# Sample attention's key dots at the output projection, its values at the memory query's projection, in a hybrid decoder layer

## The chip, the cores and the metric

One core of a Trainium2 chip runs the whole layer as one program. Its engines are TensorE (PE in the profile; PEld is its weight load), VectorE (DVE), ScalarE (ACT), GpSimd (POOL) and SyncE (SP), which issues the ordinary DMAs; gathers are issued by GpSimd. The metric is device time in microseconds (us), from the runs of the program on the chip.

## The reference, cut to what matters

The layer serves 1024 prompt tokens and 8 sample tokens with the same weights, in float32:

```
h = RMSNorm(x)
x = x + W_out(sigmoid(g1) * SSD(h) + sigmoid(g2) * RWKV7(h))
x = x + MemCrossAttn(RMSNorm(x), mem_k, mem_v)
x = x + PEER(RMSNorm(x))
```

The change is in the third line, for the samples only. Each of the 8 sample rows has a memory of its own (cache_mem_k, cache_mem_v: 256 tokens, 4 heads of 256):

```
q = (h @ w_mq).reshape(b, L, MEM_HEADS, MEM_HD)
s = einsum('blhd,bmhd->bhlm', q, mem_k) * MEM_HD ** -0.5
prob = softmax(s)
o = einsum('bhlm,bmhd->blhd', prob, mem_v)
return o @ w_mo
```

PEER picks, per token, 16 experts for each of 8 heads, and needs one row of 1024 numbers from each of two tables per expert: U for a dot with the token, V for the weighted sum.

## The kernel before, in words

The prompt goes through `front(gi)` in four groups of two blocks of 128 tokens (gi 0 to 3; the text counts them from first to fourth). A front is: input norm, the z projection (L499), the convolution stage (six weight blocks of x, B, C, L562), the SSD scan over chunks, the RWKV branch with its projections, inverse and scan (`scan`, L892), and then `rest` (L1034): output projection `project(I["w_out"][0], mT)`, memory norm, the memory query's projection (L1082), memory attention of the prompt (from L1111 on), the projection w_mo, the norm before PEER, and eight heads of the projection w_pq with the choice of experts (`Best`, L420 to L460).

The experts of the group before are worked off beside a front. A U row is a gather (L1512 on POOL) and a dot on VectorE (L1516, in two instructions, the second of which reads out the sum); a V row is a gather and a scaled addition (L1568). Both land in the pool of rows "U", seven buffers. Each row is 128 partitions of 4 KB, 0.524 MB.

The samples ride along with different groups: their memory query is projected in the second group's `rest` (into `smp["q"]`), their attention `sample_attention` (L1445) runs in the third group, and their w_mo rows and experts follow there, reading `smp["o"]`. `sample_attention` is a generator of 17 steps. The first eight each load one sample's keys in two tiles of 128 x 1024 (L1457), spread the query over the partitions with two TensorE products into the tiles pc, and make eight dots of 256 columns on VectorE (L1516, key tile w by pc, result into sat). Then the softmax (L1474 to L1480) and two tiles of probabilities, filled with zeros by GpSimd (L1486). The next eight each load one sample's values (L1457) and add four products on TensorE into pc. The seventeenth copies out the result and transposes it into `smp["o"]`.

`aside_satt(n)` (L495) takes n steps of the generator where it is called, in the third group alone. `SATT = (0, 3)` takes none per weight block of the z projection and three per block of the convolution stage, so all seventeen steps stand in the convolution stage.

Weights come as two tiles of 128 x 4 x 256 per block of 256 output columns (`weights`, L254), from the pool "w", which has five buffers. The sample's key and value tiles come from the same pool. All these loads go through SyncE in a fixed order.

What decides the order of instructions on each engine is the scheduler of the recording layer: code that stands earlier has priority, and at each point the scheduler, by its own model of durations, puts the most urgent instruction that it holds for ready. The result is a fixed order per engine; on the chip, each engine waits for its next instruction's inputs. So a front's instructions have priority over the expert rows that stand behind it in the code, and the rows fill what the scheduler takes for gaps.

Of the kernel before, what the change touches and what calls it, by code (L numbers as in the profile page):

```python
# [25 lines left out]
NQ3, NG4, NXA, NK1, NU, NUT, NVS, NW, NAC = 26, 6, 2, 5, 7, 9, 6, 5, 1  # L26
NQ3B, NSC = 5, 3
ORDER = 0
SATT = (0, 3)
MPOS = 2  # L30
SPLIT = (0,)
LATE_SLOTS = ((), tuple(range(48, 108)))
# [12 lines left out]
def decode_layer(ctx, tc, I, O):  # L45
# [33 lines left out]
    def qw():  # L79
        return t("qw", [P, 2, TMAX + NS], 4)  # L80
# [7 lines left out]
    def f2():  # L88
        return t("f2", [P, 512], 4)
# [5 lines left out]
    def pp():  # L95
        return pst("pp", 2)
# [17 lines left out]
    def copy(out, in_, scale=None, bias=None):  # L114
        if bias is not None:
            S.activation(out, in_, AF.Identity, scale=scale if scale is not None else 1.0, bias=bias)
        else:
            S.activation(out, in_, AF.Copy, scale=scale if scale is not None else 1.0)  # L118
# [71 lines left out]
    def col(name, i, n=1):  # L190
        return cols[:, spots[name] + i:spots[name] + i + n]
# [59 lines left out]
    def weights(w, c0, n=256, split=False):  # L251
        x = Weights()
        for i in range(2):
            load(x.half[i][:, :, :n], w[i * 512:(i + 1) * 512, c0:c0 + n].rearrange("(k p) c -> p k c", p=P))  # L254
        return parts(x) if split else x
# [24 lines left out]
    def parts(wt):  # L280

        def row():
            return t("U", [P, D], n_u(), F32R).rearrange("p (k x) -> p k x", k=4)

        hi, lo = [], []
        for i, w in enumerate(wt.half):
            hi.append(row())
            copy(hi[i], w)
            lo.append(row() if i else wtile(F32R))
            V.tensor_tensor(lo[i], w, hi[i].bitcast(F32), op=OP.subtract)  # L290
        return [tuple(x[k // 4][:, k % 4, :] for x in (hi, lo)) for k in range(8)]
# [30 lines left out]
    def by_channel(wt, j, h, n, p):  # L322
        for k in range(8):
            if isinstance(h, Parts):
                three(p[:, :n], [x[:, j * P:(j + 1) * P] for x in wt[k]], h.of(k, slice(0, n)), k == 0, k == 7)
            else:
                mm(p[:, :n], wt.of(k, slice(j * P, (j + 1) * P)), h[k // 2][:, k % 2, :n], k == 0, k == 7)

    def by_token(wt, h, t0, n, p, nw=256):
        for k in range(8):  # L330
            if isinstance(h, Parts):
                three(p[:n, :nw], h.of(k, slice(t0, t0 + n)), wt[k], k == 0, k == 7)
            else:
                mm(p[:n, :nw], h[k // 2][:, k % 2, t0:t0 + n], wt.of(k, slice(0, nw)), k == 0, k == 7)
# [127 lines left out]
    def front(gi):  # L462
# [12 lines left out]
        def src_x(i):  # L475
            return I["x_prompt"][0, (b0 + i) * P:(b0 + i + 1) * P, :] if i < nb else I["x_sample"][:, 0, :]
# [18 lines left out]
        def aside_satt(n):  # L495
            for _ in range(n if sc_ else 0):
                next(satt)

        for i in range(4):  # L499
            wt = weights(w_in, Z0 + i * 256, split=sa)  # L500
            aside_satt(SATT[0])
            s2 = slice(i * 256, i * 256 + 256)
            for b, (t0, n) in enumerate(body):
                p = pp()
                by_token(wt, hT, t0, n, p)
                th = f2()
                S.activation(th[:n, :256], p[:n, :256], AF.Tanh, scale=0.5)
                if b < nb:
                    V.scalar_tensor_tensor(mg[b][:n, s2], th[:n, :256], 1.0, p[:n, :256], op0=OP.add, op1=OP.mult)  # L509
                else:  # L510
                    V.scalar_tensor_tensor(th[:n, :256], th[:n, :256], 1.0, p[:n, :256], op0=OP.add, op1=OP.mult)
                    V.tensor_tensor(mg[b][:n, s2], th[:n, :256], mg[b][:n, s2], op=OP.mult)
# [48 lines left out]
        xb = [q3() for _ in range(6)]  # L561
        for i in range(6):  # L562
            wt = weights(w_in, XBC0 + i * 256, split=sa)
            aside_satt(SATT[1])
            for j in range(2):
                ct = 2 * i + j
                p = pp()
                by_channel(wt, j, hT, TT_, p)
                acc = f2()

                def cw(k):
                    return col("conv_w", k * 12 + ct)

                copy(acc[:, :TP], p[:, :TP], scale=cw(3), bias=col("conv_b", ct))
                if sa:
                    copy(smp["raw"][:, ct, :], p[:, TP:TT_])
                copy(halo[:, ct, :], p[:, TP - 3:TP])
                for k in range(3):
                    V.scalar_tensor_tensor(acc[:, 3 - k:TP], p[:, :TP - 3 + k], cw(k), acc[:, 3 - k:TP],  # L579
                                           op0=OP.mult, op1=OP.add)  # L580
                V.tensor_tensor(acc[:, 0:3], acc[:, 0:3], hc[:, ct, :], op=OP.add)
                th = f2()
                S.activation(th[:, :TP], acc[:, :TP], AF.Tanh)
                V.scalar_tensor_tensor(xb[i][:, j, :TP], th[:, :TP], 1.0, acc[:, :TP], op0=OP.add, op1=OP.mult)
        aside_satt(17)
        if last:
            p = tp()
            T.transpose(p[:36, :P], halo.rearrange("p c i -> p (c i)"), ident)
# [445 lines left out]
        def rest(bl):  # L1034
# [4 lines left out]
            mg_ = [mg[b] for b in bl] + mg[nb:]  # L1039
            body = [(i * P, P) for i in range(nl)] + ([(TP, NS)] if sm else [])  # L1040

            def project(w, src, smp_src=None):

                for i in range(4):
                    wt = weights(w, i * 256)
                    s2 = slice(i * 256, i * 256 + 256)
                    for b, (t0, n) in enumerate(body):
                        p = pp()
                        if b == nl and smp_src:
                            by_token(wt, smp_src, 0, n, p)  # L1050
                        else:
                            by_token(wt, src, t0, n, p)
                        V.tensor_tensor(mg_[b][:n, s2], p[:n, :256], mg_[b][:n, s2], op=OP.add)

            mT = [qw() for _ in range(4)]
            for b, (t0, n) in enumerate(body):
                to_cols(mg_[b][:n, :], n, mT, t0)
            for b, (t0, n) in enumerate(body):
                load(mg_[b][:n, :], src_x(bl[b] if b < nl else nb))
            project(I["w_out"][0], mT)  # L1060

            def norm(scale_cb):
                ss = t("ss", [P, 4], 4)
# [17 lines left out]
            qT = [q3() for _ in range(4)]  # L1081
            for i in range(4):  # L1082
                wt = weights(I["w_mq"][0], i * 256)
                for j in range(2):
                    p = pp()
                    by_channel(wt, j, h2, TT_, p)
                    copy(qT[i][:, j, :TP], p[:, :TP])
                    if sm:
                        copy(smp["q"][:, 2 * i + j, :], p[:, TP:TT_])
            if sm:  # L1090
                load(smp["x1"], mg_[nl][:NS, :])
                body = body[:nl]
# [630 lines left out]

    late = []
    chosen = front(0)
    sample_recurrences()
    for gi in range(1, len(GROUPS)):
        ahead = front(gi)
        z = experts(prompts(chosen), GATHERED[gi - 1])
        late += [x for i, x in enumerate(z) if i not in GATHERED[gi - 1]]  # L1730
        samples(chosen)
        chosen = ahead
# [70 lines left out]
```

## Time and profile before

| | |
|---|---|
| runs, median of 3 | 4701.04 us (4698.99 to 4721.07) |
| the profiled execution | 4729.15 us, span 4727.4 us |
| VectorE busy | 3697.7 us, 78% of the span |
| TensorE busy | 3534.4 us, 75% |
| GpSimd busy | 2501.9 us, 53% |
| ScalarE busy | 1351.2 us, 29% |
| DMA | 1369.20 MB, mean 290 GB/s; gathers (queue 0) 948.03 MB |

Busy time is time in instructions that compute; register, semaphore and DMA-issuing instructions don't count, except that GpSimd's gathers do. A busy TensorE is not TensorE at its peak, since its matmuls are pipelined. The DMA share is the mean busy share of 16 DMA engines and can read a little above 1. In the chain of waits, each piece is what the next one waited for, followed back from the last instruction; "issue" is time in which an engine waited for nothing that the profile shows.

### The profile page before, as it was taken

How to read it: one execution, taken by the hardware profiler on the slowest of the kernel's cores; microseconds unless marked ns; L12 is line 12 of the kernel's file. 1: busy time of each engine (PE TensorE's matmuls, PEld its weight loads, DVE VectorE, ACT ScalarE, POOL GpSimd, SP SyncE). 2: the span in 40 equal slices, each digit the busy share in tenths (PEclk: the TensorE clock that was granted, in tenths of full speed). 3: DMA queues.
4: the chain of work that ended last, by engine and by line, in shares of the span. 5: the costliest groups of instructions: out<-in, count | busy, mean ns of one | idle time of the engine just before them, and what ended most of it. 6: DMA issues, size and time to landing. Idle time of an engine off the chain costs nothing.

```text
span 4727.4 us, 56327 instructions
## 1 busy us (share of the span) xinstructions
PE 3534.4 (75%) x18278; PEld 2706.4 (57%) x18278; DVE 3697.7 (78%) x7765; ACT 1351.2 (29%) x3489; POOL 2501.9 (53%) x2059
## 2 busy tenths in 40 slices
PE   7889875779886786788785884387976885338998
PEld 6778764557565565366574673265655743235555
DVE  5662287998878679988886699888766797998888
ACT  5545322133123221133132221132222215233322
POOL 0000035665656645564666657855545477774664
PEclk9987877888865887788757886588757897559999
DMA  4342588899978998899989987899869878988998
GB/s 123 99 130 73 173 280 318 269 320 344 337 260 283 354 339 275 318 323 318 349 269 353 340 280 272 281 328 312 287 217 357 310 239 312 344 311 326 406 406 352
DMA packets 609103, 1369.20 MB, mean 290 GB/s; under 512 B 86124, under 2 KB 332296, under 8 KB 608800
## 3 DMA queue, kind: packets, MB, share of 16 engines
q0 software_dynamic: 260352, 948.03, 56.0%
q1 hardware_dynamic: 348456, 417.57, 26.5%
q8 instruction: 145, 2.38, 0.2%
q14 instruction: 150, 1.23, 0.1%
HBM read 1335.60 MB, written 29.90 MB: 289 GB/s over the span
## 4 chain that ended last, share of the span: by engine, by line
DVE 32%; PE 30%; DMA 15%; issue 12%; ACT 5%; POOL 5%; SPq 1%; another core or an unknown queue 0%; POOLq 0%; DVEq 0%; ACTq 0%
PE pp L112 16%; DVE U L1516 10%; PE pc L112 8%; DVE acc L1568 5%; POOL U L1512 4%; DMA U<-in_expert_v_dram,idx 4%; DMA U<-in_expert_u_dram,idx 3%; PE pg L112 2%; PE pv L112 2%; DVE q3b L450 2%; DMA w<-in_w_in_dram 1%; PE tp L112 1%; DMA q<-kt_d 1%; DVE vs L1616 1%; DVE f L579 1%
## 5 line engine op out<-in xcount | busy, mean ns | idle before, releaser
L1512 POOL DMA_INDIRECT U<-in_expert_u_dram,idx x1024 | 1298.6, 1268 | 732.4 <-issue 189.8
L1516 DVE CUSTOM_DVE_ANT_0 U<-U,xa 128x1024 f32<-128x1024 f32 x1032 | 1267.9, 1239 | 115.3 <-DMA U<-in_expert_u_dram,idx 106.5
L1512 POOL DMA_INDIRECT U<-in_expert_v_dram,idx x768 | 925.8, 1205 | 724.7 <-DVE acc L1568 183.1
L1568 DVE SCALAR_TENSOR_TENSOR acc<-U,cf,acc 128x1024 f32<-128x1024 f32 x708 | 924.0, 1305 | 98.6 <-DMA U<-in_expert_v_dram,idx 85.1
L112 PE MATMUL pp<-qw,w 128*128 128x256 f32 (+2 forms) x2872 | 745.8, 413 | 151.2 <-issue 40.9
L112 PEld LDWEIGHTS pp<-qw,w 128*128 128x128 f32 x2872 | 591.3, 218 | 277.1 <-issue 110.8
L112 PE MATMUL pp<-w,qw 128*128 128x256 f32 (+1 forms) x2528 | 633.9, 405 | 117.9 <-DVE g L509 30.0
L112 PEld LDWEIGHTS pp<-w,qw 128*128 128x128 f32 (+1 forms) x2528 | 484.5, 195 | 247.2 <-DVE g L509 34.1
L112 PE MATMUL pc<-vs,cs 128*128 128x512 f32 x510 | 200.1, 447 | 35.8 <-ACT vs L118 19.9
L112 PE MATMUL pp<-q,w 128*128 128x128 f32 (+1 forms) x1024 | 196.0, 350 | 16.6 <-DMA w<-in_w_pq_dram 8.8
L112 PEld LDWEIGHTS pp<-q,w 128*128 128x128 f32 x1024 | 169.1, 210 | 33.0 <-ACT q L118 10.5
L121 POOL TENSOR_TENSOR q3b<-q3b,q3b 128x400 f32<-128x400 f32 (+1 forms) x130 | 154.6, 1202 | 57.3 <-DVE q3b L450 55.1
L112 PE MATMUL pp<-vs,cs 128*128 128x512 f32 x510 | 172.9, 393 | 0.0
L112 PE MATMUL pc<-rst,q 64*64 64x64 f32 x1024 | 170.5, 305 | 1.6 <-issue 1.0
L112 PE MATMUL pg<-q,q 64*128 64x128 f32 (+1 forms) x384 | 108.5, 441 | 79.5 <-DMA q<-kt_d 39.9
L304 PE MATMUL tp<-ident,g 128*128 128x128 f32 (+1 forms) x296 | 62.2, 346 | 138.5 <-DVE g L1018 52.2
L112 PE MATMUL pc<-g,q 128*64 128x64 f32 x1024 | 138.8, 316 | 16.2 <-issue 12.4
L112 PEld LDWEIGHTS pc<-vs,cs 128*128 128x128 f32 x510 | 93.5, 188 | 91.0 <-ACT vs L118 36.2
L112 PEld LDWEIGHTS pg<-q,q 64*128 64x128 f32 (+1 forms) x384 | 81.6, 273 | 101.0 <-DMA q<-kt_d 42.6
L112 PE MATMUL pc<-q,q 64*128 64x128 f32 (+1 forms) x512 | 102.1, 343 | 47.7 <-ACT q L118 27.8
L304 PEld LDWEIGHTS tp<-ident,g 128*128 128x128 f32 (+1 forms) x296 | 44.0, 183 | 157.3 <-issue 55.9
L112 PEld LDWEIGHTS pc<-rst,q 64*64 64x64 f32 x1024 | 114.4, 188 | 29.9 <-issue 3.2
(506 smaller groups left out, 6336.6 us busy)
## 6 DMA issues: line engine op xcount, KB each, us to landing
w<-in_w_in_dram SPq DMA_DIRECT2D x248, 512.0 KB
U<-in_expert_v_dram SPq DMA_DIRECT2D x128, 512.0 KB
w<-in_w_pq_dram SPq DMA_DIRECT2D x80, 512.0 KB
w<-in_w_out_dram SPq DMA_DIRECT2D x40, 512.0 KB
w<-in_w_mq_dram SPq DMA_DIRECT2D x40, 512.0 KB
w<-in_w_mo_dram SPq DMA_DIRECT2D x40, 512.0 KB
U<-in_expert_u_dram,idx POOLq DMA_INDIRECT x1024
U<-in_expert_v_dram,idx POOLq DMA_INDIRECT x768
```

Source lines behind the costliest of these rows:

```text
L112: T.matmul(out, a, b, start=first, stop=last)
L121: G.tensor_tensor(out, a, b, op=op)
L304: T.transpose(p[:, j * P:j * P + n], x[:, c * P:(c + 1) * P], ident[:n, :n])
L450: V.tensor_tensor(oh[:n], iota50[:n, None, :].to_broadcast([n, 8, NCAND]), posf[:n, h, k8].unsqueeze(2).to_broadcast([n, 8, NCAND]), op=OP ...
L579: V.scalar_tensor_tensor(acc[:, 3 - k:TP], p[:, :TP - 3 + k], cw(k), acc[:, 3 - k:TP], op0=OP.mult, op1=OP.add)
L1512: G.indirect_dma_start(out=dst, out_offset=None, in_=table, in_offset=bass.IndirectOffsetOnAxis(ap=idx, axis=0))
L1516: V.tensor_tensor_reduce(out=u, in0=u, in1=x, scale=1.0, scalar=0.0, op0=OP.mult, op1=OP.add, accum_out=out)
L1568: V.scalar_tensor_tensor(z["acc"], v, cf, z["acc"], op0=OP.mult, op1=OP.add)
L1616: V.tensor_scalar(rb[:, a, :], iota, by[:, 1, t0 + a:t0 + a + 1], by[:, 2, t0 + a:t0 + a + 1], op0=OP.is_equal, op1=OP.mult)
```

## The change

All three calls of `aside_satt` in the z projection and the convolution stage go, and the numbers SATT with them. `project` gets a parameter: with it, the output projection takes two steps behind each of its four weight blocks, eight in all, which are the key steps. The memory query's projection takes two behind each of its four blocks, which are the softmax and the eight value steps, and what is left follows behind its last block. Nothing else is edited.

```diff
-SATT = (0, 3)
...
         for i in range(4):
             wt = weights(w_in, Z0 + i * 256, split=sa)
-            aside_satt(SATT[0])
             s2 = slice(i * 256, i * 256 + 256)
...
         for i in range(6):
             wt = weights(w_in, XBC0 + i * 256, split=sa)
-            aside_satt(SATT[1])
             for j in range(2):
...
-        aside_satt(17)
         if last:
...
-            def project(w, src, smp_src=None):
+            def project(w, src, smp_src=None, aside=0):
 
                 for i in range(4):
                     wt = weights(w, i * 256)
+                    aside_satt(aside)
                     s2 = slice(i * 256, i * 256 + 256)
...
-            project(I["w_out"][0], mT)
+            project(I["w_out"][0], mT, aside=2)
...
             for i in range(4):
                 wt = weights(I["w_mq"][0], i * 256)
+                aside_satt(2)
                 for j in range(2):
                     p = pp()
                     by_channel(wt, j, h2, TT_, p)
                     copy(qT[i][:, j, :TP], p[:, :TP])
                     if sm:
                         copy(smp["q"][:, 2 * i + j, :], p[:, TP:TT_])
+            aside_satt(17)
             if sm:
```

In the orders that follow, line numbers of the change lie a few below those of before (L1516 is L1515 there, L579 is L576, L1457 is L1456). ISA rows with w and sat are the key dots (the row with sat alone reads out the sum), ISA rows with U and act the U rows' dots, L1568 (L1567) the V rows.

VectorE in the convolution stage of the third group, before (L579 and L584 are the convolution, L453 and L460 the choice of experts of the second group):

```order
L584 SCALAR_TENSOR_TENSOR q_2478_13164<-f_2523_13341,f_2522_13334 128x256
L579 SCALAR_TENSOR_TENSOR f_2525_13353<-pp_13344,cols,f_2525_13353 128x253
L460 TENSOR_TENSOR gate_10585<-gate_10585,gsum_11259 128x64
L453 TENSOR_REDUCE q3b_10964<-q3b_11224 128x8
L1568 SCALAR_TENSOR_TENSOR acc_12204<-U_12928,cf_12085,acc_12204 128x1024
L453 TENSOR_REDUCE q3b_10964<-q3b_11228 128x8
L1516 ISA w_13309,sat_13186<-w_13309,pc_13314 128x256
L1516 ISA sat_13186 128x1
```

The same place of the change, at the same V row (U_12928):

```order
L576 SCALAR_TENSOR_TENSOR f_2502_13266<-pp_13257,cols,f_2502_13266 128x255
L1567 SCALAR_TENSOR_TENSOR acc_12204<-U_12925,cf_12085,acc_12204 128x1024
L459 TENSOR_TENSOR gate_10585<-gate_10585,gsum_11259 128x64
L578 TENSOR_TENSOR f_2502_13266<-f_2502_13266,hc_13154 128x3
L452 TENSOR_REDUCE q3b_10964<-q3b_11224 128x8
L452 TENSOR_REDUCE q3b_10964<-q3b_11228 128x8
L1567 SCALAR_TENSOR_TENSOR acc_12204<-U_12928,cf_12085,acc_12204 128x1024
L581 SCALAR_TENSOR_TENSOR q_2479_13165<-f_2503_13273,f_2502_13266 128x256
```

The dots are gone, and the convolution has come a column block further at the same V row. No dot is left in the stage.

SyncE from the last scan load (tx) of the third group on, before:

```order
L909 DMA tx_15842<-td_188 32x16x32 x2
L1059 DMA g_2430_12954<-in_x_prompt_dram 128x1024
L1534 DMA out_dram<-acc_17691 128x1024
L254 DMA w_16191<-in_w_out_dram 128x4x256
L1059 DMA g_2431_12955<-in_x_prompt_dram 128x1024
L254 DMA w_16214<-in_w_out_dram 128x4x256
L1557 DMA acc_24033<-x_d 128x1024
L254 DMA w_16215<-in_w_out_dram 128x4x256
L254 DMA w_16293<-in_w_mq_dram 128x4x256
```

And in the change:

```order
L905 DMA tx_15587<-td_188 32x16x32 x2
L1056 DMA g_2430_12954<-in_x_prompt_dram 128x1024
L1456 DMA w_15922<-in_cache_mem_k_dram 128x1024
L1056 DMA g_2431_12955<-in_x_prompt_dram 128x1024
L253 DMA w_15957<-in_w_out_dram 128x4x256
L253 DMA w_15958<-in_w_out_dram 128x4x256
L1456 DMA w_15961<-in_cache_mem_k_dram 128x1024
L1533 DMA out_dram<-acc_17691 128x1024
L1456 DMA w_15962<-in_cache_mem_k_dram 128x1024
L1456 DMA w_15977<-in_cache_mem_k_dram 128x1024
L1456 DMA w_15978<-in_cache_mem_k_dram 128x1024
L1556 DMA acc_24033<-x_d 128x1024
```

Key tiles now stand between the residual rows and the output weights, four for two weight tiles. The value tiles stand in the same way among the w_mq weights. Before the tx loads, the change fetches two weight tiles and three key tiles ahead, where before five weight tiles stood.

VectorE at the output projection of the third group (L1053 adds a block of it to the residual), before:

```order
L1533 SCALAR_TENSOR_TENSOR acc_17691<-acc_17691,ssf_18478,pv_18483 128x512 x2
L1053 TENSOR_TENSOR g_2430_12954<-pp_16170,g_2430_12954 128x256
L1516 ISA U_18495,act_18378<-U_18495,xa_18376 128x1024
L1516 ISA act_18378 128x1
L1516 ISA U_18498,act_18378<-U_18498,xa_18376 128x1024
```

And in the change (L1050 is the same addition):

```order
L1515 ISA U_18504,act_18378<-U_18504,xa_18376 128x1024
L1515 ISA act_18378 128x1
L1050 TENSOR_TENSOR g_2430_12954<-pp_15993,g_2430_12954 128x256
L1515 ISA U_18507,act_18378<-U_18507,xa_18376 128x1024
L1515 ISA act_18378 128x1
L1050 TENSOR_TENSOR g_2431_12955<-pp_16003,g_2431_12955 128x256
L1515 ISA w_15961,sat_15904<-w_15961,pc_15965 128x256
L1515 ISA sat_15904 128x1
```

Dots stand among the U rows, and more U rows stand between the projection's blocks. Counted over the whole order of VectorE, 38 U rows and no V row lie between the third group's last scan addition (L1018) and its first memory softmax (L1124) before, 70 U rows and 3 V rows in the change; from there to the last scaling of the norm before PEER (L1164) 42 before and 36 in the change; at the fourth group's first scan step (L910) all 776 U rows of the first three groups and the samples are done in both, and 3 V rows fewer in the change than before.

## Rows read from the trace of the kernel before

**Rows 1.** The page: the span, and busy time of each engine (share of the span).
```profile
span 4727.4 us, 56327 instructions
...
PE 3534.4 (75%) x18278; PEld 2706.4 (57%) x18278; DVE 3697.7 (78%) x7765; ACT 1351.2 (29%) x3489; POOL 2501.9 (53%) x2059
```

**Rows 2.** Busy time in stretches: start, end, length, five engines, clock, DMA, GB/s.
```profile
core 0: us, PE busy (x) PEld busy (x) DVE busy (x) ACT busy (x) POOL busy (x), PEclk, DMA share, GB/s
1868.00:2024.00 156.00, 116.19 (x297) 62.62 (x298) 144.56 (x456) 21.76 (x67) 84.17 (x73) 0.75 0.87 314
...
2509.00:2603.00 94.00, 63.20 (x262) 52.20 (x260) 49.40 (x90) 16.84 (x40) 52.12 (x41) 0.81 0.99 362
2603.00:2689.00 86.00, 65.51 (x306) 48.01 (x304) 65.00 (x122) 23.57 (x50) 59.88 (x42) 0.86 0.90 322
2689.00:2760.00 71.00, 69.02 (x328) 56.46 (x329) 57.12 (x240) 20.79 (x65) 32.68 (x29) 0.92 0.97 338
2760.00:3050.00 290.00, 144.64 (x521) 113.04 (x519) 269.27 (x761) 49.53 (x126) 210.27 (x160) 0.68 0.80 272
```

**Rows 3.** Who waited for whom, VectorE and TensorE, 1868 to 2024 us: total, times, longest.
```profile
DVE sx L1476 <- PE tp L1474: 3.4, 1, 3.4
...
PE pp L112 <- DMA w<-in_w_in_dram: 19.0, 5, 5.3
PE pg L112 <- DVE adt L541: 14.6, 1, 14.6
```

**Rows 4.** DMA issues of the sample's caches, 1800 to 2030 us: count, size of each.
```profile
w<-in_cache_mem_k_dram SPq DMA_DIRECT2D x16, 512.0 KB
w<-in_cache_mem_v_dram SPq DMA_DIRECT2D x16, 512.0 KB
```

**Rows 5.** DMA from 2509 to 2603 us: GB/s in 40 equal slices, and the total.
```profile
GB/s 272 333 335 363 407 392 403 395 355 403 390 378 368 298 295 348 346 394 411 248 91 363 314 369 336 353 400 396 397 397 394 391 397 392 394 390 403 396 393 387
DMA packets 15678, 34.04 MB, mean 362 GB/s; under 512 B 1103, under 2 KB 8818, under 8 KB 15673
```

**Rows 6.** The chain of waits, 2509 to 2689 us, longest pieces: start, length, what.
```profile
2513.74 9.01 DMA g<-in_x_prompt_dram
...
2577.57 22.03 DMA q<-kt_d
2635.28 44.08 PE pp L112 x208
```

**Rows 7.** The chain of waits, 2689 to 3050 us: shares by line.
```profile
by line: DVE U L1516 31.4%; PE pp L112 11.8%; issue 11.3%; POOL U L1512 6.7%; DMA U<-in_expert_u_dram,idx 6.7%; DVE q3b L450 4.7%; DVE q3b L453 4.1%; DVE f L579 3.3%; POOL q3b L121 2.4%; DVE q3b L421 1.7%; DVE q3b L440 1.7%; DVE q3b L424 1.
```

**Rows 8.** VectorE in order of time: start, length, instruction; two short stretches.
```profile
1862.60 1.21 DVE L1516 CUSTOM_DVE_ANT_0 U<-U,xa 128x1024 f32<-128x1024 f32 x1
1863.74 0.07 DVE L422 MATCH_VALUE_LOAD sc<-q3b,sc 128x8 f32 x1
...
1878.26 0.41 DVE L1516 CUSTOM_DVE_ANT_0 w<-w,pc 128x256 f32<-128x256 f32 x1
1878.60 0.41 DVE L1516 CUSTOM_DVE_ANT_0 w<-w,pc 128x256 f32<-128x256 f32 x1
1878.94 0.41 DVE L1516 CUSTOM_DVE_ANT_0 w<-w,pc 128x256 f32<-128x256 f32 x1
...
1879.28 1.27 DVE L1568 SCALAR_TENSOR_TENSOR acc<-U,cf,acc 128x1024 f32<-128x1024 f32 x1
1880.48 0.08 DVE L422 MATCH_VALUE_LOAD sc<-q3b,sc 128x8 f32 x1
```

**Rows 9.** Busy time in stretches: gathers alone; the late dense sum.
```profile
4100.00:4150.00 50.00, 0.00 (x0) 0.00 (x0) 42.62 (x71) 0.43 (x2) 39.17 (x36) 0.50 0.99 369
4550.00:4600.00 50.00, 46.11 (x159) 28.81 (x159) 44.48 (x67) 15.12 (x30) 30.98 (x24) 1.00 1.03 409
```

**Rows 10.** SyncE's queue in order of time, 2295 to 2330 us, during the third group's scan.
```profile
2299.68 16.67 SPq L254 DMA_DIRECT2D w<-in_w_out_dram  x5
2316.44 0.46 SPq L844 DMA_DIRECT2D td<-g  x1
```

## The prediction

> **What bounds the kernel now.** I read the page's engine table first, then the stretches, the waits, the chain of waits and the queue. The program spans 4727.4 us [rows 1], the profiled execution took 4729.15 us, and the runs have a median of 4701.04 us. No engine is full over the whole span: VectorE is busy 78%, TensorE 75% [rows 1]. So the value of a move lies in the two stretches that it joins, and the reader should look for which resource is full in each.
>
> The source is the convolution stage of the third token group, 1868 to 2024 us. There VectorE is busy 144.56 of 156 us, while the DMA engines are 0.87 full [rows 2]; what VectorE waits for is short, 3.4 us for the sample softmax the longest [rows 3]. TensorE has 116.19 us there, and its waits (19.0 us for input weights) lie beside a VectorE that is working [rows 3]. The stage is VectorE's.
>
> The destination is what follows the scan: output projection, memory norm and query projection, 2509 to 2603 us, and behind it memory attention and its projection, 2603 to 2689 us. In the first, VectorE is busy only 49.40 of 94 us, and the DMA engines are 0.99 full and move 34.04 MB at 362 GB/s [rows 2, 5]; about half of the fortieths of the stretch stand at 390 to 411 GB/s, and some dip far below [rows 5]. The chain shows TensorE's projections and two places where a transfer is late: 9.01 us for the residual rows, 22.03 us for the memory keys [rows 6]. That is a front which runs at the pace of its loads, with expert rows in every gap. Behind it, up to 2760 us, TensorE is busy 69.02 of 71 us, and from 2760 to 3050 us VectorE 269.27 of 290 us [rows 2], with a chain made largely of expert dots [rows 7].
>
> A difference of 0.5% (23.5 us) is about what a measurement of this kernel tells from no change: its three runs alone spread over 4698.99 to 4721.07 us.
>
> **The change, part by part.** Nothing is computed differently. 64 key dots, the softmax over 32 rows, 16 TensorE broadcasts, 32 value products and 32 loads of 512 KB [rows 4] leave the convolution stage for the destination. The scheduler then refills both places with expert rows, and since each engine runs its instructions in a fixed order, the order tells how many rows lie in each stretch.
>
> *Convolution stage, saved.* A dot starts 0.34 us after the one before it (1878.26, 1878.60, 1878.94) [rows 8], so 64 dots are 21.8 us of VectorE. The wait for the softmax goes, 3.4 us [rows 3]. By the order, two expert U rows and three V rows fewer stand before the third group's last scan addition (398 and 381, where 400 and 384 stood): 2 x 1.14 + 3 x 1.20 = 5.9 us by the starts in [rows 8]. Sum 31 us, all on the path, since VectorE idles only 11.4 us in the stage. Bounds: 25 us, if the five rows were hidden, and 40 us, if most of that idle time goes with them. TensorE's broadcasts and value products leave too; they lay beside VectorE and count nothing here.
>
> *Output and query projection, added.* The order puts 70 U rows and 3 V rows between the last scan addition and the first softmax of memory attention, where 38 and none stood: 35 rows more. All 32 cache tiles come into the same stretch (three are fetched ahead during the scan, in the place of three projection tiles, which then come here). 67 transfers of 0.524 MB are 35.1 MB, on top of 34.04 MB. At the stretch's own mean of 362 GB/s, 69.1 MB take 191 us, 97 more than now; at the 395 GB/s of its full fortieths [rows 5] 175 us, 81 more; at 409 GB/s, the best stretch of the late kernel [rows 9], 169 us, 75 more. I take 81: the added loads stand queued behind others, so they should fill the dips. VectorE (49 + 22 + 41 us) and TensorE stay below that time, so their part is hidden; if transfers were free, the stretch would be TensorE's chain. The Trainium skill, DMA: Bandwidth & Descriptors, section Bandwidth, gives 425 GB/s for a large load with the core alone; no stretch here shows more than 409. By it, as an estimate, the stretch would take 163 us and the forecast would fall by 12 us.
>
> *Memory attention, saved.* By the order 36 U rows stand there instead of 42. Six rows are 3.1 MB, nothing if TensorE's 44.08 us piece [rows 6] holds the pace, 10 us at the stretch's 322 GB/s. I take 4, nearer to nothing, for the chain there is TensorE's.
>
> *After it, saved and given back.* 24 U rows and the 3 V rows are now done earlier or pushed back: 27 rows less from 2689 us to the fourth group's scan. 17 of the U rows leave the stretch where TensorE is full, which had VectorE busy 57.12 of 71 us [rows 2]: they are worth between nothing and 17 x 1.14 less the 13.9 us that VectorE idles anyway, some 5. The other ten come off VectorE's full stretch at 1.2 us, 12 us. I take 17 (12 to 32, the upper bound if all 27 count). The three V rows return behind the scan, 4 us.
>
> Waits that the change adds: the cache tiles share five weight buffers with the projection weights, and one queue. Now five tiles of output weights are fetched ahead during the scan [rows 10]; afterwards two of them and three key tiles. The second block's residual rows stand behind the fourth key tile, which waits for the first dots; the transfer has waited already, so I count nothing more. What queues behind these loads on SyncE are the next weights, and TensorE's projections wait for those; it is the same transfer time, counted once. On GpSimd two fills of the probability tiles move along, beside gathers that wait for transfers.
>
> Sum: -31 + 81 - 4 - 17 + 4 = **+33 us**. Against the profiled 4729.15 us that is 4762; that execution lies 28 us above the median of the runs, and the same difference on the median gives **4734 us**.
>
> **The rivals.** *Paid back (chance 0.30).* The stretch runs at 409 GB/s (+75), memory attention gives the full 10, the later stretches the full 32 and the convolution stage its 40: 75 - 10 - 32 - 40 + 4 = -3, and up to +20 where only some of these come: 4698 to 4721, about 4709 us, no change. For it speaks that the stretch's dips look like want of requests; against it, that a stretch of gathered rows alone ran at 369 GB/s [rows 9].
>
> *Faster: the dots fall into VectorE's idle time (0.12).* VectorE idles 44.6 us in the destination, and the dots need 21.8. If the expert rows that the order adds there are issued and landed early, during the scan, the stretch has only the cache tiles more, 50.8 MB or 129 us at 395 GB/s, 35 more than now: 35 - 10 - 32 - 40 + 4 = -43, 4658 us. It decides, by 0.5%, if about 20 of the 35 rows land before 2509 us. Against it: the rows have seven buffers. The Trainium skill, Perfetto Trace Analysis, section Optimization Strategy, advises to interleave regimes whose fullest engine differs. By it the dots should move as they do here; for the 32 loads it says the reverse, as the destination's transfers are 0.99 full [rows 2].
>
> *Slots (0.12).* If five buffers, not the transfer rate, set the pace, the 43 projection and cache tiles of the stretch take 43/5 turns. A turn is the 22.03 us that a load took behind a full queue [rows 6], and some 4 us until four dots and two rows have read a key tile: 224 us instead of 175, and 4783 us. For it speaks that queue; against, that the kernel now keeps 0.99 with the same buffers.
>
> That nothing moves is excluded by the order: no dot is left in the convolution stage.
>
> **How the numbers follow.** Forecast 0.46, paid back 0.30, faster 0.12, slots 0.12. Slower by over 0.5%: 0.46 + 0.12 = 0.58; within: 0.30; faster: 0.12. The low end of the forecast's own terms is -40 + 75 - 10 - 32 + 4 = -3 (4698), the high end -25 + 97 - 0 - 12 + 4 = +64 (4765). For 8 in 10 I reach a little past both, to 4690 and 4775, which leaves out the faster case and about half of the slots.
>
> **What would show it.** After the change the convolution stage of the third group should be some 30 us shorter, with VectorE still full. From the last scan addition to the first softmax of memory attention it should take about 175 us instead of 94, with DMA at 0.95 or more and VectorE near two thirds. Behind it, fewer expert dots in the chain up to 3050 us. It is wrong if that stretch grows by less than 60 us, if its DMA share falls below 0.9 (then the slots rule), or if the later stretches give back more than 32 us.

## The result and the profile after

The change took 4746.36 us (median of 13 runs, 4721.28 to 4765.72) where the kernel before took 4715.61 us (13 runs, 4698.99 to 4727.57): ratio 1.0065, interval 1.0049 to 1.0082. That is 31 us more, or 0.65%, where 33 were forecast. The forecast time of 4734 us lies 12 us lower, because the kernel before came out at 4715.61 us over these 13 runs and not at the 4701.04 us that the forecast started from. The profiled execution took 4765.72 us, 36.6 more than that of before. Each experiment below has a ratio to the kernel before, measured beside it, and its interval in brackets.

The page's first lines after the change, to be laid beside [rows 1]:

```profile
span 4764.0 us, 56364 instructions
...
PE 3506.8 (74%) x18278; PEld 2687.0 (56%) x18278; DVE 3711.4 (78%) x7765; ACT 1351.0 (28%) x3489; POOL 2482.1 (52%) x2059
```

The whole span hardly tells the two apart: 78% of VectorE, as before. The stretches do. In order: convolution stage, output and query projection, memory attention, the products of w_pq, on which TensorE is full, and the way from their last one to the fourth group's scan:

```profile
1866.00:1993.00 127.00, 64.31 (x197) 47.73 (x197) 125.27 (x330) 20.94 (x53) 75.86 (x66) 0.69 0.76 252
2489.00:2666.00 177.00, 125.67 (x384) 70.61 (x384) 115.31 (x293) 28.85 (x73) 93.53 (x78) 0.83 0.99 374
2666.00:2746.00 80.00, 67.33 (x308) 50.42 (x308) 56.98 (x109) 18.58 (x45) 49.51 (x36) 0.86 0.94 338
2745.80:2819.80 74.00, 72.23 (x347) 58.52 (x345) 51.78 (x270) 22.52 (x67) 16.04 (x14) 0.94 0.56 189
2819.80:3403.10 583.30, 372.08 (x1640) 288.03 (x1639) 512.25 (x1233) 136.24 (x339) 370.63 (x299) 0.77 0.90 311
```

Against [rows 2], the convolution stage has shrunk from 156 us to 127 with VectorE as full as before (125.27), and the output and query projection has grown from 94 to 177 us with DMA at 0.99 as before and VectorE at 115 of 177. The transfers of that stretch, beside [rows 5]:

```profile
GB/s 286 365 404 396 401 313 328 399 390 399 411 411 395 381 364 398 387 376 389 381 407 321 309 184 190 359 403 405 396 396 396 411 405 392 396 405 410 405 402 399
DMA packets 23975, 66.23 MB, mean 374 GB/s; under 512 B 2074, under 2 KB 9242, under 8 KB 23966
```

66.23 MB instead of 34.04, and the added loads did fill dips: the mean rose from 362 to 374 GB/s. The longest pieces of the chain there:

```profile
2493.70 12.18 DMA w<-in_w_out_dram
2532.41 8.99 PE pp L111 x32
2555.87 7.48 PE pp L111 x24
2589.81 8.76 PE pc L111 x16
2608.04 17.52 DMA w<-in_w_mq_dram
2629.35 12.65 DMA w<-in_w_mq_dram
2648.79 15.47 DMA q<-kt_d
```

Four pieces are late weights or memory keys, and between them stand products of the samples (pc), which [rows 6] did not have. Who works on TensorE in the stretch, and what it waited for (line, engine, operation, tiles, shapes, count; busy, mean ns; idle before):

```profile
L111 PE MATMUL pp<-qw,w 128*128 128x256 f32 x128 | 34.6, 430 | 13.0 <-DMA w<-in_w_mq_dram 12.5 <-ACT qw L117 0.5
L111 PE MATMUL pc<-w,g 128*40 128x512 f32 x64 | 30.7, 625 | 2.5 <-DMA w<-in_cache_mem_v_dram 2.2 <-ACT g L117 0.3
L111 PE MATMUL pp<-w,qw 128*128 128x256 f32 x104 | 29.7, 448 | 9.5 <-DMA w<-in_w_out_dram 9.0 <-ACT qw L117 0.5
L111 PE MATMUL pc<-g,ident 8*128 8x512 f32 x32 | 22.2, 818 | 14.9 <-DVE sat L1515 10.6 <-DVE act L1515 4.2
```

Value products and broadcasts are 30.7 + 22.2 = 53 us of TensorE, which was busy 63 us there before and is busy 126 now.

The account of the two profiles, from the starts of the same lines (last L541, last L584, first L910, last L1018, first L1124, last L1164, and the same for the fourth group). VectorE's idle time is the length less its busy time:

| stretch | before, us | after | difference | forecast | VectorE idle, before and after |
|---|---|---|---|---|---|
| start to the third group's L541 | 1868.6 | 1866.1 | -2.5 | | 542.9, 537.2 |
| convolution stage | 154.6 | 127.2 | -27.4 | -31 | 11.4, 1.7 |
| RWKV and gates | 312.3 | 312.3 | 0.0 | | 32.4, 37.2 |
| scan | 172.9 | 183.0 | +10.1 | | 27.4, 37.9 |
| output and query projection | 95.1 | 176.9 | +81.8 | +81 | 45.1, 61.7 |
| memory attention | 84.6 | 80.3 | -4.3 | -4 | 20.5, 23.0 |
| to the fourth group's scan | 690.1 | 657.3 | -32.8 | -17 | 97.9, 93.3 |
| fourth group's scan | 187.1 | 193.9 | +6.8 | +4 | 51.0, 58.5 |
| its rest, up to the norm before PEER | 162.7 | 158.0 | -4.7 | | 58.9, 54.5 |
| the remainder | 999.4 | 1009.0 | +9.6 | | 142.1, 147.7 |

The last column is another way to read it: the span is VectorE's work and VectorE's idle time. Its idle time grew by 23 us: 17 in the projection and 10 in the scan, with 10 won in the convolution stage. The other 14 us are work: the same 7765 instructions took a little longer, for a reason that was not looked into.

Each column is one execution. The first row stands ahead of everything that the edits move, and over the fourteen profiles of this case (two kernels and twelve experiments) it took between 1853.6 and 1868.6 us; the fourth group's scan took between 173.1 and 196.7. So a difference of some 10 us in one row is not safe by itself. The two large ones are: in the seven profiles without key steps in the convolution stage, that stage took 126.8 to 127.4 us.

### The profile page after: what moved, and what is told of

Its sections match the earlier page's. It is cut to its first block, busy times and chain, and to the rows that moved or that the text cites. A ratio compares the mean times of both kernels' runs of the same rounds, so it can differ in the third digit from the quotient of the medians.

```text
span 4764.0 us, 56364 instructions
## 1 busy us (share of the span) xinstructions
PE 3506.8 (74%) x18278; PEld 2687.0 (56%) x18278; DVE 3711.4 (78%) x7765; ACT 1351.0 (28%) x3489; POOL 2482.1 (52%) x2059
## 4 chain that ended last, share of the span: by engine, by line
PE 33%; DVE 30%; DMA 16%; issue 12%; ACT 5%; POOL 4%; SPq 1%; another core or an unknown queue 1%; POOLq 0%; DVEq 0%; ACTq 0%
PE pp L111 18%; DVE U L1515 9%; PE pc L111 9%; DVE acc L1567 4%; DMA U<-in_expert_u_dram,idx 4%; POOL U L1511 4%; DMA U<-in_expert_v_dram,idx 2%; PE pv L111 2%; DVE q3b L449 2%; PE pg L111 2%; PE tp L111 1%; DMA q<-kt_d 1%; DVE vs L1615 1%; DVE f L576 1%; DVE q3b L452 1%
## 5 line engine op out<-in xcount | busy, mean ns | idle before, releaser
L1515 DVE CUSTOM_DVE_ANT_0 U<-U,xa 128x1024 f32<-128x1024 f32 x1032 | 1270.0, 1241 | 130.0 <-DMA U<-in_expert_u_dram,idx 123.4
L1567 DVE SCALAR_TENSOR_TENSOR acc<-U,cf,acc 128x1024 f32<-128x1024 f32 x708 | 929.3, 1313 | 99.0 <-DMA U<-in_expert_v_dram,idx 91.9
L111 PE MATMUL pp<-qw,w 128*128 128x256 f32 (+2 forms) x2872 | 738.1, 409 | 176.9 <-DVE f L576 79.2
L111 PE MATMUL pg<-q,q 64*128 64x128 f32 (+1 forms) x384 | 104.3, 426 | 65.8 <-ACT q L1127 32.2
```

Source lines behind the costliest of these rows:

```text
L111: T.matmul(out, a, b, start=first, stop=last)
L1515: V.tensor_tensor_reduce(out=u, in0=u, in1=x, scale=1.0, scalar=0.0, op0=OP.mult, op1=OP.add, accum_out=out)
L1567: V.scalar_tensor_tensor(z["acc"], v, cf, z["acc"], op0=OP.mult, op1=OP.add)
```

## The experiments

The theory of the prediction: dots cost VectorE's time in the source and nothing in the destination, loads cost nothing in the source and their transfer time in the destination. The rivals: another limit in the destination (TensorE's chain of broadcasts, dots and products; weight buffers), or rows refilled by the scheduler as the real cost.

**One dot of four (e2_before_few, e2_after_few).** The scores of the other heads are zeros; the same edit in both kernels.

```diff
+        V.memset(sc, 0.0)
...
-                for h in range(4):
+                for h in range(1):
```

> The kernel before with one of the four dots of each key tile. If VectorE sets the convolution stage, 48 x 0.34 = 16 us less: 0.9965 (0.995 to 0.998). If the dots lay beside other work there: 0.999 to 1.001.

> The changed kernel with one of the four dots of each key tile, the other scores set to zero once; the samples' attention is then not the reference's. 48 dots of 0.34 us are 16 us of VectorE. If VectorE's work is hidden in the output projection, the time is that of the change within 0.15% (1.005 to 1.008 of the kernel before). If the dots cost their time there: 1.003.

Before: 0.9956 (0.9930 to 0.9982). Its convolution stage took 138.4 us, 16.2 less than 154.6; 48 x 0.34 are 16.3. By the order three expert rows fewer stand before its end (3.6 us), so 12.6 to 16.2 us are the dots' own. The change: 1.0106 (1.0062 to 1.0150), not faster than the change's 1.0065. That is above both expected values, though its interval reaches down to the change's. Its stretch keeps DMA at 0.99 while VectorE's work in it falls to 96 us:

```profile
2479.00:2649.00 170.00, 127.92 (x383) 71.63 (x381) 96.10 (x192) 27.49 (x71) 87.94 (x76) 0.83 0.99 375
```

The stretch is 169.8 us, 7 less than the change's 176.9, and 2.6 MB less pass in it (63.67), which are 7 us at 374 GB/s. So the dots are paid in the source and hidden in the destination. Why this version came out slower than the change, if it did, stays open.

**A quarter of the cache loads (e1_after_quarter, e1_before_quarter).** Every tile still has its transfer and its buffer, and the dots and products keep their number and size; they read the 256 loaded columns again in place of the others.

```diff
-                load(x[m], I[name][0, b, m * P:(m + 1) * P].rearrange("p h d -> p (h d)"))
+                load(x[m][:, 0:256], I[name][0, b, m * P:(m + 1) * P, 0, :])
```

> The changed kernel, but each cache tile loads 256 of its 1024 columns: 128 KB instead of 512 KB, 12.6 MB less in all, with as many transfers, buffers, dots and products. The samples' attention output is not the reference's. By the order 84 expert rows lie between the last scan addition and the first memory softmax, where the change has 73: 66.23 - 12.6 + 5.8 = 59.4 MB. If transfer time sets that stretch: 59.4 MB at the change's 374 GB/s, 159 us instead of 177, and 11 rows less behind it, 10 to 13 us: in all some 28 us faster than the change, 1.000 to 1.003 of the kernel before. If the number of weight buffers sets it, or the dots: within 10 us of the change, 1.005 to 1.007.

> The kernel before with the same cut of the cache loads, 12.6 MB less. If VectorE sets the convolution stage, its loads were free: the time stays within 0.3% of the kernel before (0.997 to 1.001), however the order refills the stage (39 more expert rows there by its end, some 46 us of VectorE, that are missing later). If the loads of the caches cost the same time wherever they stand, 12.6 MB at 395 GB/s are 32 us: 0.993.

The change: 1.0078 (1.0050 to 1.0105), no gain; before: 1.0039 (1.0017 to 1.0061), slower. The second misses both expected values: its convolution stage, with 39 more expert rows, took 207.5 us. The first misses the value for transfers; it fits the one for buffers or dots in the stretch (within 10 us of the change), and its time lies just above that band. The stretch is 169.5 us, 7 less:

```profile
2492.00:2662.00 170.00, 127.24 (x386) 69.99 (x384) 129.07 (x317) 28.85 (x73) 111.61 (x90) 0.83 0.94 346
```

7.4 MB less (58.87 MB) would be 20 us at 374 GB/s; the stretch gave back a third of that, and DMA fell from 0.99 to 0.94. So transfers alone do not hold it. In both kernels the scheduler had also filled in rows, so the next runs held the order.

**The same with the order held (e3_after_cap, e3_after_cap_quarter, e3_before_cap_quarter).** The U rows from the 439th on are queued behind the first memory softmax:

```diff
+PINS = (('mem', 182),), ()
...
+    def behind(at, n):
+        at = [name for name, k in at if n >= k] if third[0] else []
+        return tc.issue_after(pin[at[0]]) if at else ExitStack()
...
-                u_step(state[i], k)
+                with behind(PINS[0], n):
+                    u_step(state[i], k)
```

> The changed kernel with nothing cut; the 439th and later U rows are put behind the third group's first memory softmax in each engine's order, so that 40 U rows and 3 V rows stand in the output and query projection where the change has 70 and 3. 30 rows are 15.7 MB: 66.2 - 15.7 = 50.5 MB. If transfer time sets that stretch: at 374 GB/s 135 us, 42 less than the change's 177, and the 30 rows cost 1.2 us of VectorE each behind it, 36 us, less what of VectorE's idle time they fill: in all 6 to 20 us faster than the change, 1.002 to 1.006 of the kernel before. If the chain of broadcasts, dots and value products sets it (TensorE is busy 126 us there): 160 us or more, and in all 10 to 25 us slower than the change.

> The same with cache loads of 128 KB instead of 512 KB: 12.6 MB less at nearly the same order (the samples' attention is not the reference's). 37.9 MB: by transfer time alone 101 us for the stretch; since TensorE is busy 126 us in it, not under 126, so 126 to 135 us. If the chain of broadcasts, dots and products sets it already with the whole loads: the same length as in the run with them, within 5 us, and 160 or more.

> The kernel before with cache loads of 128 KB instead of 512 KB, and the expert rows held back so that the convolution stage ends with 283 U rows and 267 V rows done, as before (the samples' attention is not the reference's). If VectorE sets the stage: its length stays within 8 us of the 154.6 us of before, and the time at 0.996 to 1.001. If its loads cost their transfer time: 32 us shorter, 0.993.

e3_after_cap: 1.0068 (1.0043 to 1.0093), the same as the change. The stretch is 159.9 us instead of 176.9, with 51.5 MB and DMA at 0.89; memory attention is 17 us longer, 97.4. With the loads cut as well: 1.0058 (1.0038 to 1.0079), and 155.8 us at 41.9 MB. So with 9.6 MB less at nearly one order, 26 us at 374 GB/s, the stretch is only 4 us shorter. The stretches come out near the expectations for TensorE's chain (160 us or more, and within 5 us of each other); the whole times fit neither expectation, since what the stretch won was paid behind it. Its last 60 us, of the whole loads and of the cut ones:

```profile
2579.00:2639.00 60.00, 57.11 (x184) 28.40 (x182) 5.62 (x12) 7.46 (x31) 5.78 (x5) 0.97 0.75 255
```

```profile
2583.00:2643.00 60.00, 57.11 (x187) 27.87 (x186) 1.55 (x5) 7.46 (x31) 0.69 (x1) 0.97 0.56 183
```

Query projection and value products keep TensorE busy 57.1 of 60 us, beside DMA at 0.75 or 0.56 and a nearly empty VectorE. So there is a second limit in the last 60 us, and with it the stretch takes 156 to 160 us, some 20 below the transfers' 177. It is not a limit of TensorE over the whole stretch: before those 60 us the DMA share was 0.91 to 1.02 with the whole loads and still 0.86 to 0.97 with the cut ones.

The third run, on the kernel before, held the count of rows but not the place of the dots: 1.0047 (1.0028 to 1.0065), and a convolution stage of 188.3 us. There VectorE is full up to 1960 us and then busy 9.92 of the last 35:

```profile
1960.00:2010.00 50.00, 30.55 (x70) 14.14 (x68) 35.43 (x65) 4.13 (x25) 21.53 (x20) 0.68 0.62 200
2010.00:2045.00 35.00, 32.97 (x118) 17.17 (x118) 9.92 (x24) 6.25 (x22) 0.58 (x2) 1.00 0.48 143
```

With its rows held back, the stage runs out of work for VectorE and ends on TensorE's products. That loads were free in the source is therefore not shown; the stage's 0.87 of DMA [rows 2] speaks for it, no run does.

**A quarter of the columns on TensorE (e5_after_cap_pe, e5_before_pe).** Broadcasts and value products of 128 columns instead of 512, in the kernel of e3_after_cap and in that of before.

```diff
-                mm(qb[i], ident[:NS, b:b + 1].to_broadcast([NS, P]), qs[:NS, i * 512:i * 512 + 512])
+                mm(qb[i][:, 0:128], ident[:NS, b:b + 1].to_broadcast([NS, P]), qs[:NS, i * 512:i * 512 + 128])
...
-                    mm(po[i][:40, :], prm[m][:, b, i, :], x[m][:, i * 512:i * 512 + 512], b == 0 and m == 0,
+                    mm(po[i][:40, 0:128], prm[m][:, b, i, :], x[m][:, i * 512:i * 512 + 128], b == 0 and m == 0,
```

> The kernel of e3_after_cap (cache loads whole, 40 U rows in the stretch) with a quarter of the columns in the samples' TensorE work: broadcasts and value products of 128 columns instead of 512 (the samples' attention is not the reference's). They were 22.2 + 30.7 us of TensorE in the change; some 40 us go. If the stretch of 160 us is set by TensorE's chain once the rows are held back: 128 to 140 us, which is 51 MB at 374 to 400 GB/s, and in all 15 to 30 us faster than e3_after_cap, 1.000 to 1.004 of the kernel before. If transfers or weight buffers already set it: 155 us or more, and the same time as e3_after_cap.

> The kernel before with the same cut of the samples' TensorE work. If VectorE sets the convolution stage, TensorE's work there was free: the stage stays at 150 us or more, 0.998 to 1.001 in all. If broadcasts and products cost their time there too: 40 us, 0.992.

e5_after_cap_pe: 1.0021 (1.0001 to 1.0040), 0.5% less than e3_after_cap, as expected if TensorE's chain sets that stretch. The stretch falls from 159.9 to 140.8 us, and DMA is full again:

```profile
2483.00:2624.00 141.00, 92.60 (x385) 70.22 (x384) 78.36 (x231) 26.90 (x70) 57.38 (x48) 0.81 0.98 363
```

That is what the transfers need: 0.89 x 159.9 = 142 us of DMA time in e3_after_cap. So the stretch has two limits, and which rules hangs on the rows put into it. The same cache tiles went through the same five buffers here, in 19 us less: with this order the buffers were not what set the 160 us.

e5_before_pe: 0.9951 (0.9930 to 0.9972), 23 us faster; forecast was no change. The convolution stage took 143.6 us instead of 154.6. By the order three V rows and two U rows fewer stand before its end, 6 us, and VectorE idles 5.4 us in it instead of 11.4. The stage is shorter than the expected 150 us or more. So TensorE's work there was nearly free, not quite; the rest of the 23 us lies outside the stage, and its cause is not settled.

**Half of the change (e4_half).**

```diff
-            aside_satt(SATT[1])
+            aside_satt((2, 2, 1, 1, 1, 1)[i])
...
-        aside_satt(17)
...
                 wt = weights(I["w_mq"][0], i * 256)
+                aside_satt(2)
```

> Half of the change: the key steps stay in the convolution stage (2, 2, 1, 1, 1, 1 per block), softmax and values go to the memory query's projection. Nothing is cut. By the order the scan ends 9 U rows later than before (+11 us of VectorE, less the softmax wait of 3.4), 65 U rows stand in the output and query projection instead of 38, with 16 value tiles: 22.6 MB more, 57 us at 395 GB/s; 36 rows fewer behind it, some 43 us at 1.2 us. In all +21 us, 1.003 to 1.006. If key dots and broadcasts in the projection are what costs: no more than 1.002.

1.0094 (1.0067 to 1.0121): not better than the whole change, and over 20 us above the forecast. The output and query projection takes 136.1 us, 41 more than before, so softmax and values, with the 27 U rows that the scheduler put beside them, are half of the 81.8. But the convolution stage wins nothing, 166.2 us with VectorE busy 162:

```profile
1863.00:2029.00 166.00, 90.78 (x237) 57.42 (x236) 161.94 (x470) 23.54 (x56) 91.36 (x81) 0.66 0.83 287
```

By this, what the stage won in the change was won by the dots; ten more expert rows (12 us) fill the place of the values.

**Two other places (e6_before_gdots, e7_scan_keys).** First the dots off VectorE, in the place of before; then the keys in the scan, where VectorE idles 27 us.

```diff
+                for i in range(2):
+                    s2 = slice(i * 512, i * 512 + 512)
+                    gtt(k[m][:, s2], k[m][:, s2], qv[:, s2], OP.mult)
...
-                    dot(k[m][:, s2], qb[h // 2][:, h % 2 * 256:h % 2 * 256 + 256], sc[:, m, b, h:h + 1])
+                    S.activation(k[m][:, s2], k[m][:, s2], AF.Copy, accum_out=sc[:, m, b, h:h + 1])
```

> The kernel before with the 64 key dots taken off VectorE: ScalarE copies the broadcast query out of PSUM, GpSimd multiplies (32 of 128 x 512), ScalarE sums. Nothing is cut. VectorE loses 64 x 0.34 = 21.8 us in a stage that it sets; GpSimd has 84 us of 156 there and gets some 32 x 1.45 = 46 us more, ScalarE some 45 us. If VectorE alone sets the stage: 0.995 to 0.997, faster than both kernels. If GpSimd's gathers, standing behind the multiplications in its order, come late: 0.999 to 1.005.

1.0050 (1.0025 to 1.0075), the upper end of what was expected for late gathers. The stage became longer, 179 us, with a VectorE that has less to do in its middle:

```profile
1916.00:1976.00 60.00, 22.32 (x82) 16.72 (x82) 43.20 (x109) 22.11 (x98) 46.40 (x39) 0.70 0.84 298
```

GpSimd took 46.6 us for the 32 multiplications, as reckoned, in the queue that also issues the rows' gathers; the longest pieces of the stage's chain are gathers of 8.47 and 9.31 us and a weight load of 10.07. That the gathers came late because of the multiplications is read from this; no run separates the two.

```diff
+                aside_satt(2)
                 tx = t("tx", [64, D], 1)
...
                 wt = weights(I["w_mq"][0], i * 256)
+                aside_satt(2)
```

> A third place for the keys: two key steps ahead of each of the four chunks of the third group's scan, softmax and values at the memory query's projection as in the change; nothing is cut. By the order 59 U rows stand in the output and query projection, where half of the change has 65 and 136 us. The convolution stage gets 28 us shorter, as in the change; the scan, with 27 us of VectorE idle and DMA 0.83 full, takes 64 dots (22 us) and 32 broadcasts: 10 to 25 us longer; the output and query projection 128 us, 33 longer; behind it 21 rows fewer, 25 us: -4 us in all, 0.996 to 1.004, the least of the moved versions. If dots among the scan's short steps hold up its chain: the scan 40 us longer or more, 1.005 or more.

1.0036 (1.0017 to 1.0056), within the expected band and the least of the moved versions, but not by the terms given. The convolution stage is 27 us shorter, as expected. The scan takes 206 us, 33 longer; its idle time was not used up but grew from 27.4 to 38.5 us. The projection takes 135.4 us, 40 longer. No version of these that computes everything is faster than the kernel before.

## Why the prediction was right, and where it was not

**Convolution stage (-31):** measured -27.4, VectorE full, but in other parts. I had counted 27.7 us of VectorE's work and 3.4 of waiting; its work fell by 17.7 us (143.2 to 125.5), since 10 us of other work came into the stage, part of it of the SSD step that follows, and its idle time by 9.7 (11.4 to 1.7). e2_before_few gives 12.6 to 16.2 us for 48 dots reckoned at 16.3. "They lay beside VectorE and count nothing", of broadcasts and products, is nearly so: e5_before_pe shows 5 us in the stage.

**Output and query projection (+81):** measured +81.8, out of two errors that cancel. I took 35.1 MB added at 395 GB/s; it was 32.2 MB at 374. The 67 transfers came as reckoned, but five tiles' worth of loads for what follows (two of w_mo, memory keys, a norm's weight) no longer fell into the stretch. VectorE was at 0.65, as said. What the term lacks is its second limit: I wrote that without transfers "the stretch would be TensorE's chain" and put no number on it. With the rows held back the stretch came to 160 us, and with 9.6 MB less on top only to 156. So the price per byte holds down to there and not much further; what free transfers would give was not run.

**Memory attention (-4):** -4.3.

**After it (-17, between 12 and 32):** -32.8, the upper bound and a little more, so that the last of my signs of being wrong (more than 32 us) came true, by less than one row. The step that failed is the price of the 17 rows in the stretch where TensorE is full [rows 2]: I gave them 5 us, as hidden beside it. Ended at the same instruction, the last of the 256 products of w_pq, that stretch has 27 U rows before and 8 after, and it took 75.9 us and 74.0. The rows did lie hidden in it. The saving came behind it, 614.2 us before against the 583.3 of the last line of the stretches above:

```profile
2688.10:2764.00 75.90, 73.38 (x349) 59.86 (x348) 61.67 (x247) 22.48 (x70) 36.99 (x30) 0.92 0.96 333
2764.00:3378.20 614.20, 397.57 (x1646) 302.16 (x1645) 530.58 (x1305) 134.63 (x338) 389.66 (x311) 0.75 0.87 298
```

In the first of the two stretches, before and after (dots of U rows; a part of the choice of experts):

```profile
L1516 DVE CUSTOM_DVE_ANT_0 U<-U,xa 128x1024 f32<-128x1024 f32 x27 | 33.7, 1254 | 5.6 <-DMA U<-in_expert_u_dram,idx 5.6
L450 DVE TENSOR_TENSOR q3b<-iota,q3b 128x400 f32<-128x400 f32 x4 | 2.9, 756 | 0.0
...
L1515 DVE CUSTOM_DVE_ANT_0 U<-U,xa 128x1024 f32<-128x1024 f32 x8 | 9.6, 1221 | 5.2 <-DMA U<-in_expert_u_dram,idx 5.2
L449 DVE TENSOR_TENSOR q3b<-iota,q3b 128x400 f32<-128x400 f32 x11 | 8.4, 789 | 0.3
```

VectorE did 24 us less of dots there and some 16 us more of other work, most of it the choice of experts, which then no longer stood behind it, where VectorE is the fuller engine (530.58 of 614.20 us, TensorE 397.57). Over both stretches 24 U rows fewer (295 and 271) took 30.9 us less of VectorE's time (365.9 and 335.0), nearly all of the 32.8. So the rows counted in full, though they lay beside a full TensorE, because other work of VectorE moved into their place. This is read from the two traces; no run tried it, and one profile of each kernel leaves the size uncertain: in e2_before_few, which has 289 U rows there, the two stretches took 670.0 us together, 20 less than before. The chain did not get fewer expert dots, as I had said it would: over 2746 to 3103 us L1515 has 31.3%, against 31.4% in [rows 7].

**The scan of the third group (no term):** +10.1. VectorE waits there for the scan's own load, and three key tiles now stand ahead of that load in SyncE's queue:

```profile
DVE tx L906 <- DMA tx<-td: 9.4, 2, 8.6
```

Before, that wait was 0.6 us. I had counted the tiles fetched ahead as a saving for the next stretch and as nothing for this one. But that the key tiles make the scan longer is not shown, and other profiles speak against it: e4_half has no key tile ahead of the scan, 2.5 us of this wait and a scan of 182.7 us; e1_after_quarter has the key tiles ahead, 1.9 us of the wait and 183.8 us. With the keys left in the convolution stage the scan took 167.6 to 183.8 us in seven profiles, with the key tiles ahead of it 178.3 to 188.5 in six. The cause of the +10 stays open.

The two unpredicted terms, -16 and +10, and the small ones behind (+3, +5) nearly cancel, so that the sum of +33 stands beside 31 in the medians. The mechanism of the two large terms was right; the exactness of the sum was in part luck, as was that of the +81.

**The rivals.** Paid back: the give-back came to its full bound, but the convolution stage gave 27 us and not 40, the stretch ran at 374 GB/s, not at 409, and the scan took 10 us of it. The Trainium skill, DMA: Bandwidth & Descriptors, section Bandwidth, has 425 GB/s for a load of 16 MB with one core alone; the best fortieth of this stretch has 411. Faster: could hardly have come as I reckoned it; e3_after_cap has 51.5 MB in the stretch, about the 50.8 of that rival, and took 159.9 us there, not 129. Slots: DMA at 0.99 speaks against it, and where the share fell to 0.89 or 0.78 TensorE was full at the end of the stretch, not waiting for buffers; e5_after_cap_pe passed all the tiles in 140.8 us. No run changed the number of buffers.

## What to carry to other kernels

A stretch with an idle engine is a place for work only if none of the resources that the work brings along is the full one there: 22 us of dots were hidden in VectorE's idle time, and the 17 MB that came with them were not. Work out the second limit of the destination too, with all that is added to it, since it can bound what a rival or a repair gives back. Work that lies hidden beside a full engine is not free where the scheduler can put other work into its place. Compare a stretch before and after between the same instructions of the engine that is full in it. And where a scheduler refills, count the work that flows into the gaps: holding 30 rows back shortened one stretch by 17 us and changed the whole by nothing.

## What was not expected of the hardware

The broadcasts are not cheaper in proportion to their columns, while the value products nearly are. At a quarter of the columns the broadcasts took 9.4 us instead of 22.2 (0.42) and the value products 9.0 instead of 30.7 (0.29), by ends that the profile models:

```profile
L112 PE MATMUL pc<-g,ident 8*128 8x128 f32 x32 | 9.4, 396 | 20.7 <-DVE sat L1520 19.8 <-issue 0.9
L112 PE MATMUL pc<-w,g 128*40 128x128 f32 x64 | 9.0, 277 | 4.8 <-DMA w<-in_cache_mem_v_dram 4.4 <-ACT g L118 0.3
```

A full share of the DMA engines is not one rate. In e3_after_cap_quarter, with its smaller loads, 269 GB/s filled 0.78 of the engines, 345 GB/s for a full share, where e3_after_cap at nearly the same order has 322 at 0.89, 362 for a full share, and the change 374 at 0.99, 378.

```profile
2487.00:2643.00 156.00, 124.34 (x384) 68.24 (x384) 79.08 (x231) 26.96 (x69) 54.42 (x48) 0.82 0.78 269
```

The Trainium skill, DMA: Bandwidth & Descriptors, section Bandwidth, says that a transfer of 64 KB reaches 138 GB/s and one of 1 MB 341. The direction is the same here, for 128 KB against 512 KB. But the size of the loads is not shown to be the cause: the convolution stage of the change, which has no such small loads, reads 252 GB/s at 0.76, 332 for a full share.
